# Accumulating weight loads, a token sum and one transposed quarter moved in a hybrid decoder layer

## The chip, the core and the metric

The kernel runs on one core of a Trainium2 chip. A core has TensorE (PE in the profile; its weight loads are PEld), VectorE (DVE), ScalarE (ACT), GpSimd (POOL) and SyncE (SP), each with its own instruction stream, and 16 DMA engines. In this kernel DMA transfers are issued from SP's, ScalarE's and GpSimd's queues. The metric is the device time of one execution in microseconds, the median over several runs.

## The reference

One layer on 256 tokens with model width D = 2048, all in float32:

```
h = rmsnorm(x)
c,b,xa,za,q,f,iv,og,ga,gb = split(h @ w_in)
ya = b * conv3(c * xa) * silu(za)              # branch A
yb = hgrn2(q, f, iv) normed per head * silu(og) # branch B
m  = sigmoid(ga) * (ya @ w_a) + sigmoid(gb) * (yb @ w_b)
x1 = x + m @ w_o
x2 = x1 + sigmoid(rmsnorm(x1) @ w_pg) * (p @ w_pp)
out = rmsnorm(x2)
```

`ga` and `gb` are 2048 columns wide each; the other eight parts of `w_in` are 1024 wide.

## The kernel before

Every product runs at more than one float32r pass: each operand is cut into a high part, rounded to float32r, and a low part, the rest (`cut`: ScalarE writes `hi`, VectorE writes `lo`). A product is then a **triple** of matmuls: hi by hi (L1038), hi by lo of the weights (L1039), lo by hi (L1040). Weights stream through SBUF in **items**: an item is 256 rows by 512 columns of a weight, split into a pair `whi`, `wlo`, and takes 12 matmuls of 512 columns (two row blocks, two halves of 128 tokens, three matmuls). Splits run some three items ahead of TensorE, into a ring of four pairs.

The main loop (`for pos, it in enumerate(items[:last_group])`) goes through the groups in this order: the projections of p, the eight narrow parts of `w_in` in two halves, then for each column quarter j = 0..3 the gates `ga` and `gb`, then `A` (by `w_a`) and `B` (by `w_b`), then `O` (by `w_o`, four column blocks of eight items), then `PG` (by `w_pg`). The framework's planner puts the instructions of each engine in an order of its own, within the dependencies; `issue_after`, `pinned` and manual dependencies bind parts of it. Each engine, and each DMA queue, then runs its stream in order.

**Seven products in place of eight.** In quarters 1, 2 and 3 the gate products of five of the eight row chunks (`SEVEN`, c = 0, 2, 3, 5, 6; kind "S", called units here) use a Strassen-like scheme over two row blocks, two token halves and the columns of `ga` and `gb`. A unit has seven triples, 21 matmuls. Three of them take plain tokens and plain or raw weights, four take sums of weight blocks or of token blocks. The other three chunks (kind "C") take the plain eight. For a unit the kernel needs:

- `sA`, the two row blocks of `ga`'s columns, and `sB`, the second row block of `gb`'s, loaded on SP's queue (L141) into two buffers each;
- `sT`, the sum X of weight blocks, which the DMA engines add up: a plain load (L157) on GpSimd's queue, then an accumulating load on the same tile (L163). There are three buffers. `add_by_dma` issues both, three times early, two items apart, in the stretch of quarter 0's `gb` (at `begun + 3, + 5, + 7`), and from then on once at the end of each `combine_weights`;
- `combine_weights(pos)`, called two items ahead of the unit: two additions into `sA` (L701), then three splits: X into `thi`, `tlo`; `sB` into `bhi`, `blo` (one buffer); the new `sA` into `thi`, `tlo`.

In this text X1 to X5 are the sums of quarter 1's five units and X6 the first of quarter 2's.

The token sums s1 to s4 are made once (`token_sums`, three groups of 1, 2 and 2 units) from x (`state["hT"]`, hi and lo) as soon as quarter 0's gates read it, and split into `shi`, `slo` (L762, L763), four tiles of 128 tokens per unit. A unit's products read x of row blocks 0 and 1 for token half 0, x of row block 1 for token half 1, and s1 to s4; nothing in quarters 1 to 3 reads x of row block 0 for token half 1 in those five chunks. `unit_products` runs the triples in the order

```
(x00, halves[0]), (x10, halves[1]), (s4, b22), (s1, t1), (s3, t3), (s2, t2), (x11, t4)
```

where b22 is the split of `sB`.

**Turning m.** The merged quarter m (L782, L786) has tokens on partitions and must have features there. `to_dram` stores it in four pieces (L304), a read-back (L315 in `turned`) brings it in block-transposed, and VectorE transposes 32 by 32 squares (L308, `square_turn`). `put_m` then splits it into `mh`, `ml` (L775, L776). Quarters 0 to 2 are parked in DRAM and come back in `unpark`; quarter 3 (`j == 3` in `ep_bb`) goes through `turned` at once, all on SP's queue, on which the loads of `w_o` (L150, 1 MB for two items, three buffers) stand too. `O` reads quarter j of m in its items c = 2j and 2j + 1.

Of the kernel before, what the change touches and what calls it, by code (L numbers as in the profile page):

```python
# [9 lines left out]
F32 = mybir.dt.float32  # L10
F32R = mybir.dt.float32r
AF = mybir.ActivationFunctionType
ALU = mybir.AluOpType
PSUM = bass.MemoryType.PSUM

P = 128
# [7 lines left out]
CW = 512  # L24
# [7 lines left out]
SEVEN = [()] + 3 * [(0, 2, 3, 5, 6)]  # L32
# [15 lines left out]
def hybrid_kernel(ctx, tc, xT, x, pT, prm, gfin, masks, w_in, w_a, w_b, w_o, w_pg, w_pp, out):  # L48
    nc = tc.nc
# [9 lines left out]
    pools, closers = {}, {}  # L59
# [13 lines left out]
    state = {"tmp": "tmp1"}  # L73
# [3 lines left out]
    def nm(s):  # L77
        uid[0] += 1
        return f"{s}_{uid[0]}"
# [16 lines left out]
    pair_sums = {}  # L96
# [9 lines left out]
    items = []  # L106
# [16 lines left out]
    def raw_of(pos):  # L123
        it = items[pos]
        if it["raw"] not in loaded:
            if it["kind"] == "S":
                t = tuple(
                    pools["st"].tile([P, n, CW], F32, tag=tag, bufs=2, name=nm(tag)) for tag, n in (("sA", 2), ("sB", 1))
                )
            else:  # L130
                t = wp.tile([P, 2, 2 * CW], F32, tag="raw", bufs=3, name=nm("raw"))
            loaded[it["raw"]] = t
        return loaded[it["raw"]]
# [18 lines left out]
    def add_by_dma(behind=None):  # L152
        pos = next((n for n, it in enumerate(items) if it["kind"] == "S" and n not in pair_sums), None)
        if pos is not None:
            w, g, c = items[pos]["w"]
            X = pair_sums[pos] = pools["st"].tile([P, 2, CW], F32, tag="sT", bufs=3, name=nm("sT"))
            d = nc.gpsimd.dma_start(out=X.rearrange("p n x -> p (n x)"), in_=w[g + 1, :, c, :])  # L157
            if behind is not None:
                tc.add_manual_dep(
                    d.ins, behind.name,  # L160
                    mybir.DependencyInfo(mybir.DependencyClass.Sync, mybir.DependencyReason.DATA), reason="order",
                )
            nc.gpsimd.dma_start(out=X, in_=w[g : g + 2, :, c, :CW].rearrange("n p x -> p n x"), accum_op=ALU.add)  # L163

    def pair_of(pool, n, tags=("whi", "wlo"), width=2 * CW):
        return tuple(pool.tile([P, width], F32R, tag=tag, bufs=n, name=nm(tag)) for tag in tags)
# [18 lines left out]
    def combine_weights(pos):  # L185
        st = pools["st"]
        (A, B), X = raw_of(pos), pair_sums[pos]
        add(A[:, 0], X[:, 0], B[:, 0])
        add(A[:, 1], A[:, 0], A[:, 1])
        ts = []  # L190
        for n, src in enumerate((X, B, A)):
            hi, lo = pair_of(st, 1, ("bhi", "blo"), CW) if n == 1 else pair_of(st, 3, ("thi", "tlo"))
# [9 lines left out]
    begun = next(n for n, it in enumerate(items) if it["kind"] == "ga" and it["last"])  # L202
# [7 lines left out]
    prm_t = const.tile([P, PRM_N], F32, name="prm_t")  # L210
    praw = pools["tmp1"].tile([P, 1024], F32, tag="X", bufs=4, name="praw")[:, : 2 * T]
    pop = pools["tmp1"].tile([P, 1024], F32R, tag="X", bufs=4, name="pop")
# [80 lines left out]
    def spread(ap, t):  # L293

        return ap.rearrange("p (b c t e) -> p t c b e", b=4, c=4, t=NT)[:, t]

    def to_dram(src, tag, bufs):  # L300
        d = dram.tile([P, 4, T], F32, tag=tag, bufs=bufs, name=nm(tag))
        to = d.rearrange("(b i) a x -> a i b x", b=4)
        for a in range(4):
            nc.sync.dma_start(out=to[a], in_=src[32 * a : 32 * a + 32, :].rearrange("i (b x) -> i b x", b=4))  # L304
        return d

    def square_turn(dst, src):
# [1 line left out]
            out=dst.rearrange("p (k a e) -> p a k e", a=4, e=32), in_=src.rearrange("p (a k e) -> p a k e", a=4, e=32)  # L309
        )  # L310

    def turned(src, lag, dst=None):
        d = to_dram(src, "turn", 3)
        yield
        nc.sync.dma_start(out=src, in_=d.rearrange("p a x -> p (a x)"))  # L315
        for _ in range(lag):
            yield
        dst = t4() if dst is None else dst
        square_turn(dst, src)
        return dst  # L320
# [379 lines left out]
    def add(out, a, b):  # L700
        nc.vector.tensor_tensor(out=out, in0=a, in1=b, op=ALU.add)  # L701
# [32 lines left out]

    def token_sums():
        nu = len(SEVEN[1])
        state["S"] = pair_of(pools["st"], 1, ("shi", "slo"), nu * 4 * P)
        state["S"] = tuple(v.rearrange("p (u s t) -> p u s t", u=nu, s=4) for v in state["S"])
        yield
        yield  # L740
        for first, n in TOGETHER:
            yield
            F, S = (
                pools["st"].tile([P, 2 * CW], F32R, tag=tag, bufs=3, name=nm(tag))[:, : n * 4 * P].bitcast(F32)
                for tag in ("thi", "tlo")
            )
            c = SEVEN[1][first]
            hi, lo = (v[:, 2 * c : 2 * (c + n), :] for v in state["hT"])
            Fv = F.rearrange("p (k t) -> p k t", t=T)
            nc.vector.tensor_tensor(out=Fv, in0=hi.bitcast(F32), in1=lo.bitcast(F32), op=ALU.add)  # L750
            yield
            Fv = F.rearrange("p (u r b t) -> p u r b t", u=n, r=2, b=2)
            Sv = S.rearrange("p (u s t) -> p u s t", u=n, s=4)
            a11, a12, a21, a22 = Fv[:, :, 0, 0], Fv[:, :, 1, 0], Fv[:, :, 0, 1], Fv[:, :, 1, 1]
            s1, s2, s3, s4 = (Sv[:, :, i] for i in range(4))
            for out, u, v, op in (
                (s1, a21, a22, ALU.subtract), (s2, s1, a11, ALU.subtract),
                (s3, a11, a21, ALU.subtract), (s4, a12, s2, ALU.add),
            ):
                nc.vector.tensor_tensor(out=out, in0=u, in1=v, op=op)  # L760
            hi, lo = (v[:, first : first + n] for v in state["S"])
            nc.scalar.activation(out=hi, in_=Sv, func=AF.Copy)  # L762
            nc.vector.tensor_tensor(out=lo, in0=Sv, in1=hi.bitcast(F32), op=ALU.subtract)  # L763
            yield

    def ep_a(j, psum):
# [11 lines left out]
    def ep_bb(j, psum):  # L778
        ga, gb = state["ga"], state["gb"]
        for t in range(NT):  # L780
            s = slice(t * CW, (t + 1) * CW)
            nc.vector.tensor_tensor(out=gb[:, s], in0=gb[:, s], in1=psum[t], op=ALU.mult)  # L782
        m = t4()
        for t in range(NT):
            s = slice(t * CW, (t + 1) * CW)
            nc.vector.tensor_tensor(out=spread(m, t), in0=blocks(ga[:, s]), in1=blocks(gb[:, s]), op=ALU.add)  # L786
        if j == 3:
            m = yield from turned(m, 3, back())
            put_m(j, m)
        else:  # L790
            state["m", j] = to_dram(m, f"m{j}", 1)
            yield

    def back():
        return pools["back"].tile([P, 1024], F32, tag="back", bufs=5, name=nm("back"))
# [259 lines left out]
    def names_of(it):  # L1055
        if it["kind"] == "C":
            return [("c", it["n"], t) for i in range(2) for t in range(NT)]
        return ["P1", ("c", 0, 0), ("c", 1, 0), "P5", "P7", "P6", ("c", 0, 1)]

    def into(name, op, part):  # L1060
        left[name] -= 1
# [3 lines left out]
    def unit_products(pos):  # L1065
        it = items[pos]
        c, h = it["c"], state["hT"]

        def x_of(r, t):
            return tuple(v[:, 2 * c + r, t * P : (t + 1) * P] for v in h)  # L1070

        hi, lo = parts.pop(pos)
        halves = [(hi[:, i * CW : (i + 1) * CW], lo[:, i * CW : (i + 1) * CW]) for i in range(2)]
        names = names_of(it)
        if it["kind"] == "C":
            for n, name in enumerate(names):
                into(name, x_of(n // 2, n % 2), halves[n // 2])
            return
        b22, t1, t3, t2, t4_ = sums.pop(pos)
        s1, s2, s3, s4 = (tuple(v[:, SEVEN[1].index(c), i] for v in state["S"]) for i in range(4))  # L1080
        for name, op, part in zip(names, (x_of(0, 0), x_of(1, 0), s4, s1, s3, s2, x_of(1, 1)),
                                  (halves[0], halves[1], b22, t1, t3, t2, t4_)):
            into(name, op, part)

    def pinned(start):
# [16 lines left out]
    for pos, it in enumerate(items[:last_group]):  # L1102
        mark = len(nc.cur_bb.bb.instructions)
        kind, j, c, last = (it[n] for n in ("kind", "j", "c", "last"))
        _, _, w, g, opname = groups[it["gi"]]
# [60 lines left out]
        else:  # L1166
            if c == 0:
                psum = [bank("s" if kind == "PP" and j >= 2 else "g") for _ in range(NT)]
            hi, lo = parts.pop(pos)
            for i in range(2):  # L1170
                k = 2 * c + i
                s = slice(i * CW, (i + 1) * CW)
# [10 lines left out]
        if pos == begun:  # L1183
            finish()
            second_part()
            active.append(token_sums())
        if pos in (begun + 3, begun + 5, begun + 7):
            add_by_dma(state["splits"][0])
        if kind == "O" and j == 0 and c == nch - 3:
            finish()  # L1190
# [23 lines left out]
    for t, halves in ((0, (0, 1)), (1, (0,)), (1, (1,))):  # L1214
        bk, n = bank("g"), CW // 2
        for c in range(nlast):
# [3 lines left out]
            hi, lo = parts[last_group + c]  # L1220
            for i in range(2):
                k = 2 * c + i
                s = slice(i * CW + halves[0] * n, i * CW + (halves[-1] + 1) * n)
# [83 lines left out]
```

## Time and profile before

| | us |
|---|---|
| runs before | 817.78, 814.62, 815.74 |
| median | 815.74 |
| the profiled execution, its own time | 816.5 |
| its span in the profile | 814.7 |
| TensorE's granted clock, share of full speed | 0.996 |

The span runs from the first to the last instruction of the profile; the 1.8 us between it and the execution's time lie around it. A row of the timeline has the start and the duration in microseconds, the engine, the line, the operation, and the tile written and those read; `x4` joins rows of one kind. Brackets tell how long the engine was idle before, and what released it. In the chain of waits, each row is a piece of the chain that ended last: start, length, what. A row of groups has busy time or durations in ns (least, median, most). A row of waits has the sum, the count and the longest, in microseconds. "issue" is time in which nothing that the profile shows was waited for.

### The profile page before, as it was taken

What the parts mean: (1) busy time and instruction counts of PE and PEld (TensorE: products, weight loads), DVE (VectorE), ACT (ScalarE), POOL (GpSimd) and SP (SyncE); (2) the same over time, 40 slices, a digit from 0 to 9 for tenths busy, and PEclk for the clock granted to TensorE, in tenths of its full rate; (3) what the DMA queues carried; (4) which work ended last, traced back from release to release, by engine and by line L of the source; (5) the groups of instructions that cost most, each with busy time, mean ns of one, the idle gap of its engine ahead of it and who ended that gap; (6) DMA issues with size and microseconds to landing.
All of it is one profiled execution on the core that took longest, in us unless ns stands there. A gap on an engine that the chain in (4) does not pass through costs nothing.

```text
span 814.7 us, 10651 instructions
## 1 busy us (share of the span) xinstructions
PE 803.2 (99%) x4059; PEld 665.4 (82%) x4059; DVE 589.2 (72%) x745; ACT 459.4 (56%) x614; POOL 48.5 (6%) x57
## 2 busy tenths in 40 slices
PE   9999999999999999999999999999999999999995
PEld 6888888888888888888888878888888788888885
DVE  7746588767766498767679968987988756677932
ACT  7576476466565466456455546556554546566623
POOL 1000000001000000010011110110100000001210
PEclk9999999999999999999999999999999999999998
DMA  9988555648867555648789989998944888777802
GB/s 339 392 307 288 197 201 175 233 139 267 252 237 249 198 175 196 207 157 269 259 296 282 286 268 297 284 280 260 283 163 177 291 300 300 255 274 298 276 34 103
DMA packets 52659, 198.52 MB, mean 244 GB/s; under 512 B 6784, under 2 KB 16256, under 8 KB 37888
## 3 DMA queue, kind: packets, MB, share of 16 engines
q1 hardware_dynamic: 45504, 180.54, 63.6%
q0 software_dynamic: 6240, 15.73, 8.2%
q10 hardware_dynamic: 864, 1.57, 0.5%
q8 instruction: 31, 0.51, 0.2%
q14 instruction: 20, 0.16, 0.1%
HBM read 184.19 MB, written 13.63 MB: 243 GB/s over the span
## 4 chain that ended last, share of the span: by engine, by line
PE 85%; DVE 7%; issue 4%; DMA 2%; ACT 2%; POOL 0%; POOLq 0%; DVEq 0%; ACTq 0%
PE g L1038 26%; PE g L1039 26%; PE g L1040 25%; DVE wlo L170 3%; PE s L1039 2%; PE s L1040 2%; PE s L1038 2%; DMA sT<-in_w_in 1%; DMA raw<-in_w_o 1%; PE s L484 1%; DVE sA L701 1%; ACT whi L169 0%; DVE tlo L170 0%; PE s L932 0%; DVE back L308 0%
## 5 line engine op out<-in xcount | busy, mean ns | idle before, releaser
L170 DVE TENSOR_TENSOR wlo<-raw,whi 128x1024 fp32r<-128x1024 f32 (+1 forms) x264 | 319.9, 1229 | 159.9 <-ACT whi L169 158.0
L169 ACT ACTIVATE whi<-raw 128x1024 fp32r<-128x1024 f32 (+1 forms) x264 | 272.9, 1051 | 208.1 <-PE g L1040 175.2
L1038 PE MATMUL g<-whi,xh 128*128 128x512 f32 (+1 forms) x738 | 283.8, 385 | 0.0
L1039 PE MATMUL g<-wlo,xh 128*128 128x512 f32 (+1 forms) x738 | 283.7, 384 | 0.0
L1040 PE MATMUL g<-whi,xl 128*128 128x512 f32 (+1 forms) x738 | 283.6, 384 | 0.0
L1040 PEld LDWEIGHTS g<-whi,xl 128*128 128x128 f32 x738 | 138.7, 188 | 27.8
L1038 PEld LDWEIGHTS g<-whi,xh 128*128 128x128 f32 x738 | 138.7, 188 | 27.5
L1039 PEld LDWEIGHTS g<-wlo,xh 128*128 128x128 f32 x738 | 138.7, 188 | 27.1
L1039 PE MATMUL g<-wlo,mh 128*128 128x512 f32 x128 | 49.9, 390 | 0.3 <-DVE wlo L170 0.3
L1038 PE MATMUL g<-whi,mh 128*128 128x512 f32 x128 | 49.6, 389 | 0.0
L1040 PE MATMUL g<-whi,ml 128*128 128x512 f32 x128 | 49.5, 389 | 0.0
L1040 PE MATMUL s<-whi,xl 128*128 128x512 f32 x84 | 32.7, 389 | 0.0
L1038 PE MATMUL s<-whi,xh 128*128 128x512 f32 x84 | 32.7, 389 | 0.0
L1039 PE MATMUL s<-wlo,xh 128*128 128x512 f32 x84 | 32.7, 389 | 0.0
L169 ACT ACTIVATE thi<-sA 128x1024 fp32r<-128x1024 f32 x15 | 15.9, 1063 | 25.0 <-DVE sA L701 21.3
L1039 PEld LDWEIGHTS g<-wlo,mh 128*128 128x128 f32 x128 | 24.0, 188 | 5.6 <-DVE wlo L170 0.7
L1038 PEld LDWEIGHTS g<-whi,mh 128*128 128x128 f32 x128 | 24.0, 188 | 5.1
L1040 PEld LDWEIGHTS g<-whi,ml 128*128 128x128 f32 x128 | 24.0, 188 | 5.0
L1039 PE MATMUL g<-wlo,ybTh 128*128 128x512 f32 x64 | 24.9, 389 | 0.0
L1040 PE MATMUL g<-whi,ybTl 128*128 128x512 f32 x64 | 24.9, 389 | 0.0
L1038 PE MATMUL g<-whi,yaTh 128*128 128x512 f32 x64 | 24.9, 389 | 0.0
L1039 PE MATMUL g<-wlo,yaTh 128*128 128x512 f32 x64 | 24.9, 389 | 0.0
(215 smaller groups left out, 910.2 us busy)
## 6 DMA issues: line engine op xcount, KB each, us to landing
raw<-in_w_in SPq DMA_DIRECT2D x66, 1024.0 KB, 5.0
raw<-in_w_o SPq DMA_DIRECT2D x16, 1024.0 KB, 6.1
raw<-in_w_pg SPq DMA_DIRECT2D x16, 1024.0 KB, 5.7
sT<-in_w_in POOLq DMA_DIRECT2D x30, 512.0 KB, 8.5
raw<-in_w_in SPq DMA_DIRECT2D x28, 512.0 KB, 6.9
raw<-in_w_a SPq DMA_DIRECT2D x8, 1024.0 KB, 6.4
raw<-in_w_b SPq DMA_DIRECT2D x8, 1024.0 KB, 7.7
turn<-t SPq DMA_DIRECT2D x60, 128.0 KB, 2.8
```

The source lines that it names most:

```text
L169: a = nc.scalar.activation(out=hi, in_=src, func=AF.Copy)
L170: v = nc.vector.tensor_tensor(out=lo, in0=src, in1=hi.bitcast(F32), op=ALU.subtract)
L484: nc.tensor.matmul(out, X[:, 0, h, s], X[:, 1, h, t], start=True, stop=True, tile_position=(0, i * n))
L701: nc.vector.tensor_tensor(out=out, in0=a, in1=b, op=ALU.add)
L1038: nc.tensor.matmul(psum, oh, hi, start=first, stop=False)
L1039: nc.tensor.matmul(psum, oh, lo, start=False, stop=False)
L1040: nc.tensor.matmul(psum, ol, hi, start=False, stop=last)
```

## The change

1. `sB` gets three buffers in place of two, `sT` four in place of three.
2. `add_by_dma` issues the plain load of a new X first and then the accumulating load of the X before it, behind that plain load on GpSimd's queue. It is called four times early in place of three (also at `begun + 9`).
3. The fourth token sum s4 is no longer kept in `shi`, `slo`: its split is written into x's place, row block 0, token half 1 of the unit's chunk. The split of the sums becomes two: three quarters into `shi`, `slo`, one into x.
4. In a unit, the product with b22 and s4 goes first.
5. `to_dram` and `turned` take the queue as an argument, and quarter 3 of m is stored and read back on GpSimd's queue.

```diff
-                    pools["st"].tile([P, n, CW], F32, tag=tag, bufs=2, name=nm(tag)) for tag, n in (("sA", 2), ("sB", 1))
+                    pools["st"].tile([P, n, CW], F32, tag=tag, bufs=bufs, name=nm(tag))
+                    for tag, n, bufs in (("sA", 2, 2), ("sB", 1, 3))
...
-            X = pair_sums[pos] = pools["st"].tile([P, 2, CW], F32, tag="sT", bufs=3, name=nm("sT"))
+            X = pair_sums[pos] = pools["st"].tile([P, 2, CW], F32, tag="sT", bufs=4, name=nm("sT"))
             d = nc.gpsimd.dma_start(out=X.rearrange("p n x -> p (n x)"), in_=w[g + 1, :, c, :])
...
-            nc.gpsimd.dma_start(out=X, in_=w[g : g + 2, :, c, :CW].rearrange("n p x -> p n x"), accum_op=ALU.add)
+        if "adding" in state:
+            w, g, c = items[state["adding"]]["w"]
+            X = pair_sums[state.pop("adding")]
+            with tc.issue_after(d.ins) if pos is not None else ExitStack():
+                nc.gpsimd.dma_start(
+                    out=X, in_=w[g : g + 2, :, c, :CW].rearrange("n p x -> p n x"), accum_op=ALU.add
+                )
+        if pos is not None:
+            state["adding"] = pos
...
-    def to_dram(src, tag, bufs):
+    def to_dram(src, tag, bufs, queue=nc.sync):
...
-            nc.sync.dma_start(out=to[a], in_=src[32 * a : 32 * a + 32, :].rearrange("i (b x) -> i b x", b=4))
+            queue.dma_start(out=to[a], in_=src[32 * a : 32 * a + 32, :].rearrange("i (b x) -> i b x", b=4))
...
-    def turned(src, lag, dst=None):
-        d = to_dram(src, "turn", 3)
+    def turned(src, lag, dst=None, queue=nc.sync):
+        d = to_dram(src, "turn", 3, queue)
         yield
-        nc.sync.dma_start(out=src, in_=d.rearrange("p a x -> p (a x)"))
+        queue.dma_start(out=src, in_=d.rearrange("p a x -> p (a x)"))
...
-        state["S"] = pair_of(pools["st"], 1, ("shi", "slo"), nu * 4 * P)
-        state["S"] = tuple(v.rearrange("p (u s t) -> p u s t", u=nu, s=4) for v in state["S"])
+        state["S"] = pair_of(pools["st"], 1, ("shi", "slo"), nu * 3 * P)
+        state["S"] = tuple(v.rearrange("p (u s t) -> p u s t", u=nu, s=3) for v in state["S"])
...
-            hi, lo = (v[:, first : first + n] for v in state["S"])
-            nc.scalar.activation(out=hi, in_=Sv, func=AF.Copy)
-            nc.vector.tensor_tensor(out=lo, in0=Sv, in1=hi.bitcast(F32), op=ALU.subtract)
+            sums_of = tuple(v[:, first : first + n] for v in state["S"])
+            fourth = tuple(v[:, 2 * c : 2 * (c + n) : 2, P:] for v in state["hT"])
+            for (hi, lo), src in ((sums_of, Sv[:, :, :3]), (fourth, Sv[:, :, 3])):
+                nc.scalar.activation(out=hi, in_=src, func=AF.Copy)
+                nc.vector.tensor_tensor(out=lo, in0=src, in1=hi.bitcast(F32), op=ALU.subtract)
...
-            m = yield from turned(m, 3, back())
+            m = yield from turned(m, 3, back(), nc.gpsimd)
...
-        return ["P1", ("c", 0, 0), ("c", 1, 0), "P5", "P7", "P6", ("c", 0, 1)]
+        return [("c", 1, 0), "P1", ("c", 0, 0), "P5", "P7", "P6", ("c", 0, 1)]
...
-        s1, s2, s3, s4 = (tuple(v[:, SEVEN[1].index(c), i] for v in state["S"]) for i in range(4))
-        for name, op, part in zip(names, (x_of(0, 0), x_of(1, 0), s4, s1, s3, s2, x_of(1, 1)),
-                                  (halves[0], halves[1], b22, t1, t3, t2, t4_)):
+        s1, s2, s3 = (tuple(v[:, SEVEN[1].index(c), i] for v in state["S"]) for i in range(3))
+        s4 = x_of(0, 1)
+        for name, op, part in zip(names, (s4, x_of(0, 0), x_of(1, 0), s1, s3, s2, x_of(1, 1)),
+                                  (b22, halves[0], halves[1], t1, t3, t2, t4_)):
...
-        if pos in (begun + 3, begun + 5, begun + 7):
+        if pos in (begun + 3, begun + 5, begun + 7, begun + 9):
             add_by_dma(state["splits"][0])
```

## The prediction

> **What bounds the kernel now.** The page comes first, for the busy shares, then the busy time by stage (length, then busy time of TensorE, its weight loads, VectorE, ScalarE, GpSimd).
>
> ```profile
> span 814.7 us, 10651 instructions
> PE 803.2 (99%) x4059; PEld 665.4 (82%) x4059; DVE 589.2 (72%) x745; ACT 459.4 (56%) x614; POOL 48.5 (6%) x57
> ```
> ```profile
> 0.00:20.00 20.00, 18.54 (x72) 13.62 (x73) 14.03 (x22) 15.39 (x26) 2.11 (x12) 1.00 0.91 337
> 460.00:480.00 20.00, 18.95 (x84) 15.34 (x84) 15.42 (x17) 11.74 (x14) 3.55 (x4) 1.00 0.77 209
> 640.00:660.00 20.00, 19.71 (x87) 15.95 (x87) 12.98 (x13) 10.10 (x13) 0.00 (x0) 1.00 0.93 331
> 800.00:815.00 15.00, 5.99 (x50) 5.79 (x49) 3.01 (x7) 3.31 (x8) 0.56 (x1) 0.78 0.34 123
> ```
>
> TensorE sets the time. All of its 11.5 idle us (814.7 - 803.2) lie in these four stretches: 1.46 in the first, 1.05 and 0.29 in the two in the middle, the rest behind the last matmul. The change touches neither end. The timeline of TensorE shows the two holes in the middle: start, length, and in brackets the idle time before and what ended it.
>
> ```profile
> 474.79 0.39 PE L1038 MATMUL s<-bhi,shi 128*128 128x512 f32 x1
> 476.23 0.50 PE L1039 MATMUL s<-blo,shi 128*128 128x512 f32 x1 [1.04 <-DVE blo L170]
> 476.56 0.40 PE L1040 MATMUL s<-bhi,slo 128*128 128x512 f32 x1
> ...
> 646.84 0.61 PE L1038 MATMUL g<-whi,mh 128*128 128x512 f32 x2
> 647.74 0.50 PE L1039 MATMUL g<-wlo,mh 128*128 128x512 f32 x1 [0.29 <-DVE wlo L170]
> 648.08 0.40 PE L1040 MATMUL g<-whi,ml 128*128 128x512 f32 x1
> ...
> 650.15 0.40 PE L1038 MATMUL g<-whi,mh 128*128 128x512 f32 x1
> ```
>
> Matmuls otherwise start some 0.227 us apart (two take 0.61 where one takes 0.39; more digits from six whole items below). So the first hole costs 476.23 - 474.79 - 0.227 = 1.21, and the slow start behind it (476.56 - 476.23 - 0.227) 0.1: **1.32 us**. In the second, two matmuls begin at 646.84, so the next was due at 647.29: 0.45, and 0.11 behind it: **0.56 us**. The most that this change can win is 1.32 + 0.56 = **1.88 us**, 0.23% of the time. I take 0.5%, 4.1 us, as what a measurement of this kernel can tell from no change, so the profile all but excludes a clear gain.
>
> The chain of waits and the timelines of GpSimd and VectorE name the cause of the first hole.
>
> ```profile
> 452.07 0.29 issue
> 452.36 0.59 POOL sT L157
> ...
> 461.51 11.32 DMA sT<-in_w_in
> ...
> 475.57 0.61 DVE blo L170
> ```
> ```profile
> 442.23 0.59 POOL L157 DMA_DIRECT2D sT<-in_w_in  x1 [0.81 <-DVE tlo L170]
> 449.80 1.18 POOL L163 DMA_DIRECT2D sT<-in_w_in  x1 [6.97 <-DMA sT<-in_w_in]
> 452.36 0.59 POOL L157 DMA_DIRECT2D sT<-in_w_in  x1 [1.38 <-DVE tlo L170]
> 461.51 1.18 POOL L163 DMA_DIRECT2D sT<-in_w_in  x1 [8.56 <-DMA sT<-in_w_in]
> ```
> ```profile
> 473.02 0.69 DVE L701 TENSOR_TENSOR sA<-sT,sB 128x512 f32<-128x512 f32 x1 [4.48 <-DMA sT<-in_w_in]
> ```
>
> The fifth weight sum, X5, is loaded at 452.36, as its buffer comes free; the accumulating load on top of it (L163) has to wait until that load has landed, goes at 461.51, and lands 11.3 us later, at 472.83. VectorE sat idle for it from 468.54 to 473.02, and blo, near the end of that chain, came 1.04 us late.
>
> **The loads and the accumulation.** With four buffers X5 takes X1's buffer and not X2's, so its plain load goes where the fourth went, at 442.23. Its accumulation goes right behind the plain load of X6, which waits for X2's buffer as X5's did: at 452.36 + 0.59 = 452.95 in place of 461.51, 8.6 us sooner. By then X5's load is 10.7 us old, more than the 7.6 and 9.2 us that the two loads above took. With the same 11.3 us X5 lands at 464.3, before VectorE has done its earlier work at 468.54, so X5 no longer ends a wait. Queued behind GpSimd's waits are only more loads of X; each accumulation still needs its own load, as before. The bytes are the same, but one more transfer of half a megabyte can be under way beside SP's weight loads. If crowding makes X5's 11.3 us longer by 8.6, the hole stays as it is; short of 4.2 (468.54 - 464.3) nothing of it is left. Bounds 0 and -1.32; I take **-1.32**, as the two loads above differ by 1.6 us only.
>
> **b22 first.** The product with blo goes from the third triple to the first, so bhi and blo are needed two triples, 6 x 0.227 = 1.36 us, sooner in each of 15 units. The tightest unit that I found beside X5's:
>
> ```profile
> 457.44 0.69 DVE L170 TENSOR_TENSOR blo<-sB,bhi 128x512 fp32r<-128x512 f32 x1
> ...
> 460.05 0.39 PE L1039 MATMUL s<-blo,shi 128*128 128x512 f32 x1
> ```
>
> blo is made at 458.13 and used 1.92 us later; 0.56 would stay. The pair has one buffer, so its next filling waits for the b22 product of the unit before, and that too comes 1.36 us sooner. In X5's unit blo was ready at 476.18, without the idle 4.48 at 471.7, and the unit starts at 474.79 - 1.36 = 473.43. So 0; with that cover gone, at most 1.36. The third sB buffer frees SP of waits for blo, but sA, loaded beside it, keeps its own: 0.
>
> **The token sum in x's place.** Each of three splits becomes two, of three quarters and of one. No product is added or removed.
>
> ```profile
> 431.29 0.43 DVE L760 TENSOR_TENSOR tlo<-tlo,thi 128x256 f32<-128x256 f32 x1
> 433.51 1.23 DVE L763 TENSOR_TENSOR slo<-tlo,shi 128x1024 fp32r<-128x1024 f32 x1 [1.13 <-ACT shi L762]
> ```
> ```profile
> 432.42 1.06 ACT L762 ACTIVATE shi<-tlo 128x1024 fp32r<-128x1024 f32 x1 [3.91 <-DVE tlo L760]
> 473.90 0.61 ACT L169 ACTIVATE bhi<-sB 128x512 fp32r<-128x512 f32 x1
> ```
>
> VectorE's rows give (1.23 - 0.43)/768 = 1.04 ns an element and 0.16 us fixed, so three instructions more cost 0.5 us; ScalarE's give 0.16 fixed, 0.5 us too. What hides them is the lead of the weight splits, which wait for a buffer that TensorE still reads, not for time:
>
> ```profile
> ACT whi L169 <- PE g L1040: 178.5, 119, 4.4
> ```
>
> So 0, and 0.5 with the lead gone. The write into x waits for matmuls of the quarter before, which have run.
>
> **The last quarter's turn on GpSimd.** This part can lose. SP's issues and landing, then VectorE and ScalarE:
>
> ```profile
> 637.33 1.78 SPq L304 DMA_DIRECT2D turn<-t  x4
> 639.21 0.39 SPq L150 DMA_DIRECT2D raw<-in_w_o  x1
> 642.84 0.34 SPq L315 DMA_DIRECT2D t<-turn  x1
> ```
> ```profile
> t<-turn SPq DMA_DIRECT2D x1, 512.0 KB, 4.1
> ```
> ```profile
> 637.22 4.62 DVE L170 TENSOR_TENSOR wlo<-raw,whi 128x1024 fp32r<-128x1024 f32 x4
> 646.46 1.23 DVE L170 TENSOR_TENSOR wlo<-raw,whi 128x1024 fp32r<-128x1024 f32 x1 [2.54 <-ACT whi L169]
> 647.60 1.24 DVE L308 STREAM_TRANSPOSE back<-t 128x1024 f32<-128x1024 f32 x1
> ```
> ```profile
> 648.88 1.07 ACT L775 ACTIVATE mh<-back 128x1024 fp32r<-128x1024 f32 x1 [0.78 <-DVE back L308]
> ```
>
> SP issues four stores, then a weight load at 639.21 whose buffer the first of the four wlo freed at some 637.22 + 1.23 = 638.45, then waits for the stores and reads back at 642.84. Without the turn on SP that load goes 0.77 us sooner, with it the split at 646.46, whose lateness is the second hole: **-0.56**, or nothing if the load is slower under more traffic.
>
> The turn took from 637.33 to 646.9 (642.84 + 4.1). GpSimd starts 0.29 us behind its releaser and needs 0.59 an issue (chain above); a read-back of half a megabyte I price by its loads where traffic is light:
>
> ```profile
> 565.87 0.59 POOL L157 DMA_DIRECT2D sT<-in_w_in  x1 [10.15 <-DVE tlo L170]
> 570.86 1.18 POOL L163 DMA_DIRECT2D sT<-in_w_in  x1 [4.40 <-DMA sT<-in_w_in]
> ```
>
> That is 5.0 us from issue to landing, 7.6 and 9.2 in the dense stretch. So: start at 637.6, four issues to 640.0, landing 3.7 later as SP's did (642.84 - 639.11), read-back at 643.7, landed at 648.7 to 652.9. The transpose began at 647.60, so it comes 1.1 to 5.3 us late; I take 1.5, near the light end, as SP's own read-back met 4.1 here.
>
> The page DMA: Bandwidth & Descriptors of the Trainium skill (Latency and other measured facts) gives about 1 us to the first byte on GpSimd's queue and 0.6 on SP's, and its section on issuing engines puts plain transfers on SP. By it the two hops cost 0.8 us more, an estimate, and the transpose would still be late.
>
> Behind the transpose on VectorE stand further weight splits and ml. The matmul that waits starts at 650.15, with mh done at 649.95: 0.2 us of slack, and closing the second hole moves TensorE 0.56 sooner. In unchanged order it stalls 1.5 - 0.2 + 0.56 = 1.9 us, and the change as a whole comes out at 0. But the order isn't the program's:
>
> ```profile
> L1038 PE MATMUL g<-whi,mh x128: 388/389/395, 630.5 to 717.5; 128*128 128x512 f32 x128
> ```
>
> From 630.5 to 646.84 run six items of 12 matmuls (16.34/72 = 0.227). The seventh, in program order the first on this quarter, ran 646.84 to 650.15, before mh was there; so an item of the next column block was put in its place. A second one would cover 2.72 us. Whether it is, the trace of before can't show. Bounds 0 (covered) and 5.7 (landed at 652.9, uncovered); between 0 and the 1.9 of the middle delay I take half, **+0.9**.
>
> **Sum.** -1.32 - 0.56 + 0.9 = -1.0 us on the profiled execution's 816.5 (the span and 1.8 around it): 815.5. It stands 0.8 above the median of the runs, 815.74, which becomes **814.7**.
>
> **Rivals.** A: both holes close and the turn is covered: -1.88, 813.9. For it, the order bends around this quarter already; against it, the slower queue. B: the turn costs what the rest wins or somewhat more, 0 to +1.5, about 816.5. For it, 0.2 us of slack at mh. C, slower: the read-back on GpSimd meets weight loads that now go sooner (the engines' share is 0.93 in that window) and takes X5's 11.3 us. It lands at 655.0, the transpose is 7.4 late, VectorE holds the splits behind it, and TensorE stalls 7.4 + 0.36 = 7.8: +5.9 net, 821.6, or 818.9 with one item as cover. It decides from a delay of 1.5 us, where the gain is used up, and passes 0.5% from 5.6. Against it, SP's 4.1 at the same place. D: crowding delays X5 and the first hole stays: -0.56 + 0.9, 816.1; against it 4.2 us to spare.
>
> **How the numbers follow.** Forecast 0.40, A 0.20, B 0.18, C 0.14, D 0.08. Of C 0.10 lies above 0.5%, and 0.02 of the forecast goes to a reordering elsewhere that I can't see; a clear gain gets 0.02, out of A, since no row has room for it. The range runs from 813.3 (A and half a microsecond of spread) to 818.6 (the covered end of C).
>
> **What would show it.** Right: an L163 some 0.6 us behind an L157 for X5 and no wait for sT on VectorE; no idle before a bhi or blo matmul; the weight load at about 638.5; the read-back near 643.7 and the transpose 1 to 2 us later than 647.6. Wrong: idle before blo still there, a hole of over 2 us before a matmul on mh or ml, or new holes among the sums between 440 and 600.

## The result: 1.6 us slower, and the profile after

| | before | after |
|---|---|---|
| median, us | 815.74 | 817.33 |
| lowest to highest | 814.62 to 818.74 (19 runs) | 816.81 to 818.26 (19 runs) |
| the profiled execution / its span | 816.5 / 814.7 | 817.66 / 815.9 |

The ratio is 1.0019, with a 95% interval of 1.0012 to 1.0026: the changed kernel is 1.0 to 2.1 us slower. The forecast was 814.7, a microsecond faster. The time lies in the predicted range and within the 0.5% that were called no change, but it went the other way, which these runs can tell: their interval is only 1.1 us wide.

First the page of the changed kernel, then its busy time in the two stretches with the holes (columns as before; the last three are TensorE's granted clock, the busy share of the DMA engines and GB/s).

```profile
span 815.9 us, 10662 instructions
PE 803.6 (98%) x4059; PEld 664.5 (81%) x4059; DVE 590.1 (72%) x748; ACT 458.6 (56%) x617; POOL 51.1 (6%) x62
```
```profile
460.00:480.00 20.00, 20.00 (x89) 16.19 (x88) 17.88 (x19) 11.96 (x14) 3.61 (x4) 1.00 1.03 317
640.00:660.00 20.00, 17.91 (x78) 14.16 (x77) 11.26 (x10) 7.53 (x8) 0.56 (x1) 1.00 0.92 341
```

The idle time moved. The stretch at 460 lost TensorE 1.05 us before and now loses nothing that the busy time shows; the stretch at 640 lost 0.29 and now loses 2.09. TensorE's timeline has the places.

```profile
473.67 0.39 PE L1049 MATMUL s<-bhi,xh 128*128 128x512 f32 x1
474.05 0.50 PE L1050 MATMUL s<-blo,xh 128*128 128x512 f32 x1
474.39 0.40 PE L1051 MATMUL s<-bhi,xl 128*128 128x512 f32 x1
...
646.09 0.39 PE L1049 MATMUL g<-whi,mh 128*128 128x512 f32 x1
647.03 0.50 PE L1050 MATMUL g<-wlo,mh 128*128 128x512 f32 x1 [0.55 <-DVE wlo L179]
647.37 0.40 PE L1051 MATMUL g<-whi,ml 128*128 128x512 f32 x1
...
651.74 0.39 PE L1049 MATMUL g<-whi,mh 128*128 128x512 f32 x1
653.67 0.50 PE L1049 MATMUL g<-whi,mh 128*128 128x512 f32 x1 [1.54 <-ACT mh L786]
654.00 0.39 PE L1050 MATMUL g<-wlo,mh 128*128 128x512 f32 x1
```

With the same working as before (start less the start before less 0.227, and the slow one behind it): 0.27 us is left of the hole before blo, the one before wlo is 0.82, and a new one of **1.81** stands before the first matmul that needs the last quarter of m. The chain of waits leads from there straight back to the turn; its DMA pieces are the time from an issue to the landing.

```profile
637.39 7.95 DMA turn<-t x2
...
645.88 5.38 DMA t<-turn
...
652.56 1.07 ACT mh L786
```

VectorE's and GpSimd's timelines, and SP's, whose loads are one group from 627.23 on, with the three that fall beside the stores seen singly in narrow windows:

```profile
470.84 0.69 DVE L710 TENSOR_TENSOR sA<-sT,sB 128x512 f32<-128x512 f32 x1
...
651.28 1.25 DVE L317 STREAM_TRANSPOSE back<-t 128x1024 f32<-128x1024 f32 x1 [2.67 <-DMA t<-turn]
```
```profile
451.92 0.58 POOL L158 DMA_DIRECT2D sT<-in_w_in  x1 [8.32 <-DVE tlo L179]
452.49 1.24 POOL L168 DMA_DIRECT2D sT<-in_w_in  x1
...
636.81 2.25 POOL L313 DMA_DIRECT2D turn<-t  x4 [65.52 <-DVE t L797]
645.88 0.56 POOL L324 DMA_DIRECT2D t<-turn  x1 [6.82 <-DMA turn<-t]
```
```profile
627.23 21.74 SPq L151 DMA_DIRECT2D raw<-in_w_o  x6
...
637.67 0.33 SPq L151 DMA_DIRECT2D raw<-in_w_o  x1
...
639.94 0.33 SPq L151 DMA_DIRECT2D raw<-in_w_o  x1
...
643.20 0.33 SPq L151 DMA_DIRECT2D raw<-in_w_o  x1
```

X5's accumulation (L168, 452.49) goes 0.57 us behind a plain load, as the prediction had it, and VectorE no longer waits for X5. The turn took the time back: the stores were issued by 639.06, the last of them landed only at 645.34 (637.39 + 7.95 in the chain), the read-back went at 645.88, and the transpose began at 651.28 where it had begun at 647.60. While the stores were under way, SP sent three loads of 1 MB. In the kernel before, SP sent the first behind the stores (639.21) and the second only behind the read-back too (643.27, right after the read-back at 642.84).

### The profile page after: what moved, and what is told of

It is laid out like the page before. It is cut to its first block, busy times and chain, and to the rows that moved or that the text cites. A ratio compares the mean times of both kernels' runs of the same rounds, so it can differ in the third digit from the quotient of the medians.

```text
span 815.9 us, 10662 instructions
## 1 busy us (share of the span) xinstructions
PE 803.6 (98%) x4059; PEld 664.5 (81%) x4059; DVE 590.1 (72%) x748; ACT 458.6 (56%) x617; POOL 51.1 (6%) x62
## 4 chain that ended last, share of the span: by engine, by line
PE 90%; DVE 3%; issue 2%; DMA 2%; ACT 2%; POOL 0%; POOLq 0%
PE g L1049 27%; PE g L1051 27%; PE g L1050 27%; PE s L1050 3%; PE s L1049 3%; PE s L1051 3%; DVE wlo L179 2%; DMA turn<-t 1%; DMA t<-turn 1%; DVE back L317 1%; PE s L493 1%; ACT mh L786 1%; DMA praw<-in_pT 0%; ACT whi L178 0%; PE s L594 0%
```

## The experiments

The first four share 29 runs of the kernel before (median 815.59), the last four 17 (815.57). The numbers of theories in the expectations: 4 is that the first hole is there in some executions only and that the new load order trims these, 5 that the turn is late because weight loads that SP's order used to keep behind it now share the engines with it, 6 that GpSimd's queue is itself slow.

**The changed kernel with the turn back on SP.**

```diff
-            m = yield from turned(m, 3, back(), nc.gpsimd)
+            m = yield from turned(m, 3, back())
```

> The changed kernel with the last quarter's turn back on SP's queue, all else as changed. Theory 1 (the turn on GpSimd costs some 2.1 us, the rest of the change wins what the first hole cost): 2 us under the changed kernel, about 815.2, 0.5 under the kernel before; no idle before the first matmul on the last quarter, the hole before blo gone, the hole before wlo at about 647 of some 0.5 us back. Theory 3 (the loss lies in another part: the split of the token sums, b22 first, the order of the loads): 817 or more, and a hole of 1 us or more somewhere between 440 and 600.

Measured: 815.57 (815.03 to 816.46, 11 runs), ratio 0.9995 (0.9987 to 1.0004). Its SP and VectorE timelines:

```profile
626.54 2.60 SPq L151 DMA_DIRECT2D raw<-in_w_o  x2
635.85 1.79 SPq L313 DMA_DIRECT2D turn<-t  x4
637.74 0.39 SPq L151 DMA_DIRECT2D raw<-in_w_o  x1
641.41 0.34 SPq L324 DMA_DIRECT2D t<-turn  x1
641.84 7.47 SPq L151 DMA_DIRECT2D raw<-in_w_o  x3
```
```profile
646.61 1.25 DVE L317 STREAM_TRANSPOSE back<-t 128x1024 f32<-128x1024 f32 x1 [0.42 <-DMA t<-turn]
```

Taking the turn off GpSimd alone gives the 1.8 us back (817.33 - 815.57). All the rest of the change together is worth nothing that can be measured: the interval, -1.1 to +0.3 us, doesn't hold the 1.32 that theory 1 had it win. The two traces also split the lateness. Loads of `w_o` run 0.69 us earlier here (626.54 against 627.23 for the first in that stretch), so the transpose at 646.61 corresponds to 647.30 there: the turn on GpSimd is 3.98 us later. Of that, the start of the stores makes 0.27 (636.81 - 635.85 - 0.69), the four issues 0.46 (2.25 - 1.79), the read-back 0.20 (5.40 against 5.20), and the wait between the last issue and the read-back **3.05**: 6.82 (639.06 to 645.88) against 3.77 (637.64 to 641.41). Most of this wait is the landing of the last store, at 645.34 against 641.27, which makes 2.65; from landing to read-back GpSimd took 0.54 and SP 0.14, the other 0.40. The start, the issues and this last step, 1.1 us in all, go with GpSimd's queue; the landing is what the next experiments are about.

**The kernel before with only the turn on GpSimd.**

```diff
-    def to_dram(src, tag, bufs):
+    def to_dram(src, tag, bufs, queue=nc.sync):
...
-    def turned(src, lag, dst=None):
+    def turned(src, lag, dst=None, queue=nc.sync):
...
-            m = yield from turned(m, 3, back())
+            m = yield from turned(m, 3, back(), nc.gpsimd)
```

> The kernel before with only the last quarter's turn put on GpSimd's queue. Theory 1: about 2.1 us above the kernel before, 817.9, with a hole of 1.5 to 2 us before the first matmul on the last quarter and the 1.2 us hole before blo still there. Theory 3: within 0.7 us of the kernel before.

Measured: 817.8 (817.06 to 821.12, 12 runs), ratio 1.0027 (1.0015 to 1.004): +2.2 us. The same lateness stands in GpSimd's timeline, without any other part of the change:

```profile
637.01 2.23 POOL L304 DMA_DIRECT2D turn<-t  x4 [52.26 <-DVE t L786]
645.96 0.56 POOL L315 DMA_DIRECT2D t<-turn  x1 [6.72 <-DMA turn<-t]
```

The read-back goes 6.72 us after the last issue (639.24 to 645.96). A surprise stands at the other place, in VectorE's and TensorE's timelines:

```profile
471.08 0.69 DVE L701 TENSOR_TENSOR sA<-sT,sB 128x512 f32<-128x512 f32 x1 [1.82 <-DMA sT<-in_w_in]
```
```profile
475.55 0.39 PE L1038 MATMUL s<-bhi,shi 128*128 128x512 f32 x1
475.78 0.39 PE L1039 MATMUL s<-blo,shi 128*128 128x512 f32 x1
```

This is the old load order, yet VectorE waited 1.82 us for X5 in place of 4.48, and there is no hole before blo. The first hole isn't in every execution.

**Half of the turn on GpSimd: the stores, or the read-back.** Two edits of the changed kernel, the first in `turned`, the second in its call of `to_dram`:

```diff
-        queue.dma_start(out=src, in_=d.rearrange("p a x -> p (a x)"))
+        nc.sync.dma_start(out=src, in_=d.rearrange("p a x -> p (a x)"))
```
```diff
-        d = to_dram(src, "turn", 3, queue)
+        d = to_dram(src, "turn", 3)
```

> The changed kernel, the four stores of the last quarter on GpSimd, the read-back on SP. If the stores' landing is what is late (6.8 us after the last issue in the changed kernel, 3.7 on SP before): the transpose still starts 2.5 us or more after 647.6 of the kernel before, and the time is within 0.7 us of the changed kernel. If the read-back on GpSimd is what is late, the time falls by 1 us or more.

> The changed kernel, the four stores on SP, the read-back on GpSimd. If the stores' landing is what is late: the read-back goes near 642.5, the transpose starts within 1.5 us of the kernel before, and the time falls by 1.5 to 2 us, to about 815.5. If the read-back is what is late: within 0.7 us of the changed kernel.

Measured with the stores on GpSimd: 816.14 (815.03 to 818.35, 10 runs), ratio 1.0005 (0.9996 to 1.0014). The time fell by 1.2, which the expectation gave to the read-back, while the transpose came 5.3 us after 647.6, which it gave to the stores; so the time alone can't decide here, and the trace has to. The stores are as late (the read-back goes at 645.25), but the planner put another item in front of the quarter, and the transpose came at 652.92 without a wait of its own. The holes that are left come from a weight load that landed late, as ScalarE's timeline shows:

```profile
645.49 2.00 ACT L178 ACTIVATE whi<-raw 128x1024 fp32r<-128x1024 f32 x2 [3.70 <-DMA raw<-in_w_o]
```

Measured with the read-back on GpSimd: 823.22 (822.87 to 823.95, 4 runs), ratio 1.0086 (1.0073 to 1.0099). VectorE's and TensorE's timelines:

```profile
650.19 1.25 DVE L317 STREAM_TRANSPOSE back<-t 128x1024 f32<-128x1024 f32 x1 [7.58 <-DMA t<-turn]
651.36 2.32 DVE L179 TENSOR_TENSOR wlo<-raw,whi 128x1024 fp32r<-128x1024 f32 x2
```
```profile
652.60 0.79 PE L1050 MATMUL g<-wlo,mh 128*128 128x512 f32 x1 [5.20 <-DVE wlo L179]
653.19 0.63 PE L1051 MATMUL g<-whi,ml 128*128 128x512 f32 x1
653.61 0.63 PE L1049 MATMUL g<-whi,mh 128*128 128x512 f32 x1
```

Here the stores land as on SP (read-back at 641.70), and the read-back itself takes 8.5 us, with three loads of 1 MB sent beside it (637.89, 639.42 and 642.64). Neither forecast held. The planner put the transpose ahead of two weight splits; VectorE stood at it for 7.58 us, and TensorE waited 5.20 for a split. So neither half alone has the price of the whole: what each costs hangs on the order that the planner makes around it.

**The kernel before once more**, for a second profiled execution of it:

> The kernel before, profiled once more. The run with the turn alone on GpSimd, which has the same instructions up to the last quarter, showed no hole before blo: VectorE waited 1.8 us for the fifth sum there, 4.5 in the profile of before. Theory 4 (the first hole is there in some executions only, with the landing of the fifth sum): the wait on VectorE is another, the hole some length between 0 and 1.2 us, and the execution's time goes with it. Rival (the hole is a fixed cost of this program, 1.2 to 1.3 us): the hole is there with 1.1 to 1.4 us.

Measured: 815.13 in one run, span 813.2. VectorE's timeline, and TensorE's at blo:

```profile
471.07 0.69 DVE L701 TENSOR_TENSOR sA<-sT,sB 128x512 f32<-128x512 f32 x1 [2.23 <-DMA sT<-in_w_in]
```
```profile
474.83 0.39 PE L1038 MATMUL s<-bhi,shi 128*128 128x512 f32 x1
475.05 0.39 PE L1039 MATMUL s<-blo,shi 128*128 128x512 f32 x1
```

The same program, with a wait of 2.23 for X5 and no hole before blo, as the first half of theory 4 has it; of the second hole 0.28 is left. The first profiled execution had 1.88 us of holes and was 816.5.

**The changed kernel with its weight loads held behind the turn.** The turn stays on GpSimd; the loads for the next items of `O` wait until the read-back has landed.

```diff
-                nc.sync.dma_start(out=raw, in_=w[g, :, c : c + 2, :])
+                d = nc.sync.dma_start(out=raw, in_=w[g, :, c : c + 2, :])
+                if it["kind"] == "O" and it["j"] == 1 and c < 4:
+                    tc.add_manual_dep(
+                        d.ins, state["read"].name,
+                        mybir.DependencyInfo(mybir.DependencyClass.Sync, mybir.DependencyReason.DATA), reason="order",
+                    )
...
-        queue.dma_start(out=src, in_=d.rearrange("p a x -> p (a x)"))
+        state["read"] = queue.dma_start(out=src, in_=d.rearrange("p a x -> p (a x)")).ins
```

> The changed kernel, with the two loads of w_o that share the stretch with the turn (column block 1, first two loads) held until the read-back has landed. Only the landing of the turn is read from it; the time must rise by several us, since the loads come late. Theory 5 (crowding: GpSimd's transfers land late because the weight loads, sent sooner, share the engines): the last store lands within 4 us of its issue, in place of 7.3, and the read-back within 5 us. Theory 6 (the queue itself is slow for these transfers): the stores land 6 us or more after the last issue as in the changed kernel.

Measured: 817.98 in one run, span 816.2. GpSimd, SP, VectorE and TensorE in turn (lines stand up to five lower in this kernel):

```profile
636.59 2.25 POOL L318 DMA_DIRECT2D turn<-t  x4 [65.52 <-DVE t L802]
642.24 0.56 POOL L329 DMA_DIRECT2D t<-turn  x1 [3.40 <-DMA turn<-t]
```
```profile
645.80 1.28 SPq L151 DMA_DIRECT2D raw<-in_w_o  x3
```
```profile
645.77 1.25 DVE L322 STREAM_TRANSPOSE back<-t 128x1024 f32<-128x1024 f32 x1 [2.83 <-DMA t<-turn]
```
```profile
645.64 0.39 PE L1056 MATMUL g<-whi,ml 128*128 128x512 f32 x1
648.16 0.50 PE L1054 MATMUL g<-whi,mh 128*128 128x512 f32 x1 [2.13 <-ACT mh L791]
```

The queue is the same, and nothing big runs beside the turn: the read-back goes 3.40 after the last issue in place of 6.82 and lands in 3.53 in place of 5.40, and the transpose comes 5.5 us sooner than in the changed kernel. That is crowding, and it refutes theory 6 as the main cause. What stays on GpSimd without the loads is the 2.25 for four issues and the 0.54 from landing (641.70) to read-back. The time rose by 0.65, not by several us as was forecast, and isn't won back: TensorE came to the last quarter at 645.64 + 0.23 = 645.87, 6.1 us sooner than in the changed kernel (651.74 + 0.23 = 651.97), and waited 2.13 for mh. The likely reason, not tested, is that the planner had fewer loaded items to put in front of the quarter.

**The changed kernel with the turn on ScalarE's queue**, which is a hardware queue like SP's:

```diff
-            m = yield from turned(m, 3, back(), nc.gpsimd)
+            m = yield from turned(m, 3, back(), nc.scalar)
```

> The changed kernel with the turn's five transfers on ScalarE's queue: off SP as in the change, weight loads as early, but a hardware queue. Theory 5: the stores land as late as on GpSimd, 6 us or more after the last issue, and the time stays above 816.5. Theory 6: they land within 4 us, the transpose starts within 1 us of 647.6, and the time is 815.6 or less, as with the turn on SP or a little under it. ScalarE, which waits in order, may hold up a split at the read-back; that would show as a wait of ScalarE for the stores.

Measured: 821.81 (821.07 to 822.9, 5 runs), ratio 1.0072 (1.005 to 1.0094). The chain of waits, then TensorE:

```profile
637.57 6.04 DMA turn<-t
...
643.70 6.50 DMA t<-turn
```
```profile
648.72 0.39 PE L1051 MATMUL g<-whi,ml 128*128 128x512 f32 x1
652.61 0.80 PE L1049 MATMUL g<-whi,mh 128*128 128x512 f32 x1 [3.50 <-ACT mh L786]
653.20 0.63 PE L1050 MATMUL g<-wlo,mh 128*128 128x512 f32 x1
653.63 0.63 PE L1049 MATMUL g<-whi,mh 128*128 128x512 f32 x1
```

With no software queue in it, the last store takes 6.04 us (5.6 from the end of its issue, a little under what was expected) and the read-back 6.50, with SP's loads sent beside them at 637.34, 639.61 and 642.81. So both queues that were tried in place of SP's make the turn late, as they free SP's loads. It costs more than on GpSimd because the quarter is needed one item sooner, at 648.95, and because matmuls run slowly for a while behind so long a hole.

**The old load order in the changed kernel, turn on SP**: three `sT` buffers, each accumulation behind its own plain load, three early calls; the token sum in x's place, b22 first and three `sB` buffers stay.

```diff
-            X = pair_sums[pos] = pools["st"].tile([P, 2, CW], F32, tag="sT", bufs=4, name=nm("sT"))
+            X = pair_sums[pos] = pools["st"].tile([P, 2, CW], F32, tag="sT", bufs=3, name=nm("sT"))
...
-        if "adding" in state:
-            w, g, c = items[state["adding"]]["w"]
-            X = pair_sums[state.pop("adding")]
...
+            nc.gpsimd.dma_start(out=X, in_=w[g : g + 2, :, c, :CW].rearrange("n p x -> p n x"), accum_op=ALU.add)
...
-            m = yield from turned(m, 3, back(), nc.gpsimd)
+            m = yield from turned(m, 3, back())
...
-        if pos in (begun + 3, begun + 5, begun + 7, begun + 9):
+        if pos in (begun + 3, begun + 5, begun + 7):
```

> The turn on SP and the old order of the loads of the sums (three buffers, each accumulation behind its own load, three early calls); b22 first, the third sB buffer and the token sum in x's place stay. Theory 4: the median is within 0.5 us of 815.6 and the runs spread up to 817.5 or more again, as the kernel before's do, where the kernel with the new order and the turn on SP stayed under 816.5. Rival (the new order wins nothing and the spread is chance): median and spread as with the new order.

Measured: 815.27 (814.84 to 816.13, and one run at 821.06, 12 runs), ratio 1.0 (0.9984 to 1.0016). In VectorE's timeline X5's sum isn't even waited for:

```profile
468.43 0.69 DVE L702 TENSOR_TENSOR sA<-sT,sB 128x512 f32<-128x512 f32 x1
```

The load order wins nothing that can be measured in the median, and the second half of theory 4 finds no support here: apart from the one run, the times spread by 1.3 us, as with the new order (1.4). Whether the new order trims the longer executions that the kernel before has now and then stays open. Runs more than 1.5 us above the fastest of their set were 16 of 65 with the kernel before and 1 of 12 here; with the new order they were none of 30 with the changed kernel and with its turn on SP, but 4 of 10 with the stores on GpSimd. No version was found that beats both kernels; those with the turn on SP equal the kernel before.

**One table closes the account.** Holes are summed from TensorE's timeline as above, between 360 and 790 us, with the slow matmuls behind them.

| profiled execution of | span | holes | span less holes |
|---|---|---|---|
| before | 814.7 | 1.9 | 812.8 |
| before again | 813.2 | 0.3 | 812.9 |
| after | 815.9 | 2.9 | 813.0 |
| after, turn on SP | 813.7 | 1.0 | 812.7 |
| before, turn on GpSimd | 816.3 | 3.0 | 813.3 |
| stores on GpSimd | 815.0 | 2.0 | 813.0 |
| read-back on GpSimd | 822.2 | 9.3 | 812.9 |
| loads held | 816.2 | 3.5 | 812.7 |
| turn on ScalarE | 820.0 | 7.0 | 813.0 |
| old load order | 813.2 | 0.4 | 812.8 |

The last column varies by 0.6 while spans vary by 9: to within that, the holes are the whole story of these executions, and no step of the change costs time anywhere else.

## Why the prediction went wrong, point by point

**Two steps failed, with about equal weight.** Between the forecast, 814.7, and the measured 817.33 lie 2.6 us. The loads and the accumulation were to win 1.32, and all of the change without the turn measured -0.02: 1.3 us of the miss. Moving the turn off SP was to cost 0.34 net (+0.9 and -0.56) and cost 1.76 (817.33 - 815.57): 1.4 us. Either miss alone would have used up the forecast gain.

**The landing of the turn was mis-sized.** The prediction had the stores "landing 3.7 later as SP's did (642.84 - 639.11), read-back at 643.7"; the read-back went 6.8 after the last issue, at 645.88, as the last store landed only at 645.34. It priced SP's landing under SP's order, although its own next-door term says that without the turn on SP the weight load goes sooner. That load, and the two behind it (639.94 and 643.20), are what the stores then shared the engines with; with them held, the read-back went 3.4 after the last issue. The start and the issues on GpSimd were priced well (637.6 to 640.0 forecast, 636.81 to 639.06 measured), and so was the read-back (5.0 forecast, 5.4 measured). The transpose came 3.7 late (651.28 against 647.60), not 1.5. A second item was put ahead, as the text held possible: the matmul on the last quarter was due at 651.74 + 0.23 = 651.97. Even so 1.81 of it showed. The term of +0.9 measured +1.8 (against the changed kernel with the turn on SP) and +2.2 (alone on the kernel before).

**The term of -0.56 came out as +0.26.** The weight load was to go at 638.5 and went at 637.67, so the cause was read rightly. The load met the turn's transfers, as the prediction's "or nothing if the load is slower under more traffic" allowed: it was sent 1.54 us sooner than before and landed 0.71 sooner (644.55 against 645.26), as it took 6.9 us in place of 6.1. TensorE, with the first hole gone, was there 0.98 sooner, so the hole grew. ScalarE's timeline of the changed kernel:

```profile
644.66 1.06 ACT L178 ACTIVATE whi<-raw 128x1024 fp32r<-128x1024 f32 x1 [2.75 <-DMA raw<-in_w_o]
```

The hole before wlo is 0.82 now; it was 0.56, and 0.28 in the second execution of the kernel before.

**The term of -1.32 was right in mechanism and wrong as a term of the median.** The accumulation goes 8.7 us sooner (452.49 against 461.51), X5 is there in time, and 1.05 of the 1.32 is gone in the profiled execution. But of four profiled executions with the old load order, the kernel before twice, that with the turn alone on GpSimd, and that with the old order restored, only the first had that hole. The prediction noted that its execution stood 0.8 above the median and still took off both, the hole and the 0.8. What put that execution above the median was in part the hole itself, since all spans agree once the holes are taken off. With 812.9 for a span without holes and 1.9 around it, the kernel before can at best become some 814.8, where its fastest runs lie (814.62), and its median had only some 0.9 to lose. All of the change without the turn measured -0.02 (ratio 0.9987 to 1.0004).

**Sum on the profiled executions:** forecast -1.32 - 0.56 + 0.9 = -1.0; measured -1.05 + 0.26 + 1.81 = +1.0, where the spans differ by 1.2. One figure of the range doesn't follow from the working: its upper end, 818.6, is called the covered end of C, which the prediction worked out as 818.9.

**What was right.** b22 first, the token sum in x's place and the third sB buffer at 0: all but 0.27 us at blo is gone (and that too with the turn on SP), and with them and without the turn the time is that of the kernel before. Rival B, which had the turn cost what the rest wins or up to 1.5 more, is the nearest to what happened, with 1.6; it deserved more than 0.18, since the price of the turn was the one number that no row of the kernel before showed under the new traffic. Rival C's mechanism, VectorE held at a late transpose with splits queued behind it, came in full only with the read-back alone on GpSimd, at +7.6 us.

## What to carry to other kernels

A queue's order is also a priority: to move a small transfer that waits onto another queue frees the big loads behind it to run beside it, so ask of such an edit what it releases before asking what the new queue costs. Price a transfer under the traffic that the edit makes, not under that of the profile before. A hole in one profiled execution is a term of the median only if other executions have it too.

## What the runs showed of the hardware

**Landing depends on the company more than on the queue.** The four 128 KB stores had landed, counted from the end of the last issue, in 2.9 us on GpSimd with no big load beside them, 3.6 on SP in its order, and 6.3 on GpSimd and 5.6 on ScalarE's hardware queue beside 1 MB loads. The 512 KB read-back took 3.5, 5.2, 5.4 and 6.5 in the same four kernels (3.6 to 4.1 in three other executions with the turn on SP), and 8.5 when it alone was on GpSimd. The queue shows in the first store, which met least traffic: 2.4 us from issue to landing on GpSimd and 2.1 on SP and ScalarE, a difference of 0.4, as the prediction's estimate had for each hop. The Trainium skill's page DMA: Bandwidth & Descriptors (Issuing engines are not separate DMA queues) says that transfers from all queues run on the same 16 engines and interleave. The landings beside loads of another queue agree. It has the spreading of transfers over queues save issue time only; here it also took away an order that was worth about 2 us.

**A hole has a second price once it is long.** Behind holes of 0.2 to 2.3 us one matmul at most is slow, by 0.11. Behind the two long ones, 3.7 us in the kernel with the turn on ScalarE's queue and 5.4 with the read-back on GpSimd, matmuls start 0.43 us apart, as the rows from 653.20 and from 653.19 show, and take up 0.227 again only at 658.64 and 658.20: some 2.9 and 2.7 us more. The Trainium skill's page TensorE: Matmul & The Clock Gate (Part 1: The HAM clock gate) has TensorE fall to half its clock after a window of about 3.4 us without work, and stay there for about as long once busy. Both traces have the half clock, but not these lengths: the granted clock is 0.50 from 651.67 to 658.49 and from 651.25 to 658.07, 6.8 us in both. It fell 2.6 and 3.9 us after the last matmul had ended (649.11 and 647.40), and TensorE worked for 5.9 and 5.5 us before it came back. With the loads held, 2.13 us without a matmul left the clock at 1.00. Rival C of the prediction, a stall of 7.8 us, had no term for this, and the slow stretch makes up 43% and 30% of what the spans of those two kernels lost (2.9 of 820.0 - 813.2, and 2.7 of 822.2 - 813.2).
